# Gate and up products of 18 of 22 feature tiles made as seven block products in place of eight

## The chip, the cores and the metric

The kernel runs on one core of one Trainium2 chip. The metric is the device time of one execution in microseconds (us), the median of three runs.

## The reference

Two layers work on a state x of 512 tokens by 1024 features in float32. Each layer adds a mixer (four kinds of attention, gated and projected) and then a gated feed-forward network (FFN). The change touches the FFN alone:

```python
def rms_norm(x, g):
    y = x * lax.rsqrt(jnp.mean(x * x, axis=-1, keepdims=True) + RMS_EPS)
    return y * g

for l in range(2):
    h = rms_norm(x, g_pre_mix[l])
    x = x + rms_norm(hybrid_mixer(h, ...), g_post_mix[l])
    h = rms_norm(x, g_pre_ffn[l])
    f = (silu(h @ w_ffn_gate[l]) * (h @ w_ffn_up[l])) @ w_ffn_down[l]
    x = x + rms_norm(f, g_post_ffn[l])
```

`w_ffn_gate` and `w_ffn_up` are 1024 x 2816 and `w_ffn_down` is 2816 x 1024, so the hidden layer has 22 tiles of 128 features. `RMS_EPS` is 1e-6.

## The kernel before

State and hidden values lie feature-major: a tile is 128 features (partitions) by 512 tokens. Every float32 product is made of three products of a narrower type: an operand is split into a rounded part (hi) and the rest (lo), and `mm3` (lines 305 to 308) issues hi by hi, hi by lo and lo by hi into one PSUM bank. One feature tile of the gate or the up product (`fm`) takes 8 tiles of 128 input features, so 24 matmuls of 128 x 128 weights by 512 columns.

The weights stream in units of 128 x 1024 float32. `w_load` (line 238) issues the DMAs on SyncE (SP) into three raw buffers. `conversion` makes hi on ScalarE (line 271) and lo = raw - hi on VectorE (line 272), in two halves of 512, into two pools of four buffers; `take` hands a unit to TensorE while two more are being converted. PSUM has eight banks under two tags, `acc` and `b`, four each.

`out_block` ends with a stretch ordered by hand (`ordered(True)`), in which the first five FFN products (gate and up of tiles 0 and 1, gate of tile 2) are begun while the norm of the new state is still being formed; line 1379 makes the last of them. After it the tile scheduler sets the order, from the order of the code and the buffers.

`ffn` (lines 1385 to 1413) goes over the 22 feature tiles. The gate product in PSUM is multiplied by the norm's factors `rB` (line 1390, VectorE), goes through Silu (line 1391, ScalarE), is multiplied by `rB` again (line 1392, GpSimd: the factor of the up product), then by the up product (line 1409, VectorE), and is split into hi (line 298, ScalarE) and lo (line 299, GpSimd). The splits of all 22 tiles stay in memory until the down product: in layer 0 `down_block` goes through the 8 output tiles one after the other (`columns`, `full_column`), in layer 1 `finish` makes token-major columns of 256 with lines 792 to 794. In layer 1 `to_tokens` also transposes the state on TensorE (line 1421, copied out of PSUM by ScalarE, line 1424) in the background of the FFN.

```python
def silu(z, s, ps, rb):
    nc.vector.tensor_mul(z, ps, rb)
    nc.scalar.activation(s, z, AF.Silu)
    nc.gpsimd.tensor_mul(s, s, rb)
...
            nc.vector.tensor_mul(s, s, up)
            pr = keep(s)
            self.split_to(pr[0], pr[1], s, lo_engine=nc.gpsimd)
```

Of the kernel before, what the change touches and what calls it, by code (L numbers as in the profile page):

```python
# [17 lines left out]
S = 512  # L18
# [30 lines left out]
SQ = 3  # L49
LAST_K = ((0, 2), (2, 2), (4, 2), (6, 2), (8, 4), (12, 4), (16, 4), (20, 2))  # L50

# [6 lines left out]
def plan():  # L58
# [6 lines left out]
    for l in range(LAYERS):  # L65
# [27 lines left out]
        for m in range(FT):  # L93
            for key in ("w_ffn_gate", "w_ffn_up"):
                add(key, 8, 128, lambda a, l=l, m=m, key=key:
                    _ktiles(a[key][l], 0, 8, np.arange(m * 128, m * 128 + 128)))
        if l < LAYERS - 1:
            for d in range(8):
                for k0, nk in ((0, 8), (8, 8), (16, 6)):
                    add("down", nk, 128, lambda a, l=l, d=d, k0=k0, nk=nk:  # L100
                        _ktiles(a["w_ffn_down"][l], k0, nk, np.arange(d * 128, d * 128 + 128)))
# [92 lines left out]
class Builder:  # L194
# [28 lines left out]
    def stream_init(self):  # L223
# [5 lines left out]
        self.raw, self.whl = {}, {}  # L229

    def w_load(self, upto):
        while self.n_dma <= min(upto, len(self.plan) - 1):
            i = self.n_dma
            _, nk, nc, _ = self.plan[i]
            n = nk * nc

            t = self.a() if i < 2 else self.wraw.tile([128, 1024], F32, tag="raw", name="raw")
# [5 lines left out]
    def w_conv(self, upto):  # L243

        while self.n_conv <= min(upto, len(self.plan) - 1):
            for f in self.conversion():
                f()

    def conversion(self, lo_engine=None):
# [7 lines left out]
        if name == "held":  # L257
            tiles = [(self.ar(), self.ar()) for _ in range(2 if nk * ncol > 512 else 1)]
            if len(tiles) == 1:
                kh = nk  # L260
# [19 lines left out]
    def take(self, name, ahead=None):  # L280
# [4 lines left out]
        return self.whl.pop(i)  # L285

# [64 lines left out]
    def rms(self, ss, nt=4):  # L351

        r, steps = self.rms_steps(ss, nt)
# [4 lines left out]
    def rms_steps(self, ss, nt=4):  # L358
        v, r, t = (self.small(nt) for _ in range(3))

        def steps():
            self.nc.vector.tensor_scalar(v, ss[:, 0:nt], 1.0 / D, RMS_EPS, op0=ALU.mult, op1=ALU.add)
            yield
            yield from self.root(v, r, t)
# [482 lines left out]
    def next_factors(self, ss):  # L847
        self.rT = self.rms(ss)
# [300 lines left out]
    def columns(self, name, xs, gain, n):  # L1149

        nc = self.nc
        y, acc = [], None
        for d in range(n):
            ps = self.full_column(name, xs)
# [7 lines left out]
    def down_block(self, xs, gain, x, next_gain):  # L1162
# [29 lines left out]
        def sums(half):  # L1192
            ss[half] = self.token_sums(acc, None, 2 * half, 2)
            r[half], chain[half] = self.rms_steps(ss[half], 2)
# [190 lines left out]
    def ffn(self, l, u, ps):  # L1385
# [3 lines left out]
        def silu(z, s, ps, rb):  # L1389
            nc.vector.tensor_mul(z, ps, rb)  # L1390
            nc.scalar.activation(s, z, AF.Silu)  # L1391
            nc.gpsimd.tensor_mul(s, s, rb)  # L1392

        def keep(s):
# [203 lines left out]
```

## Time and profile before

| what | value |
|---|---|
| median of 3 runs | 1745.59 us (1744.67 to 1745.9) |
| the profiled execution, by its own clock | 1747.27 us |
| span of its profile | 1745.4 us, mean granted TensorE clock 0.994 |
| TensorE busy | 1711.2 us (98%), 9044 matmuls |
| VectorE, ScalarE, GpSimd busy | 915.2, 730.1, 468.2 us |
| moved by DMA | 179.01 MB, mean 103 GB/s |
| FFN products taken out of PSUM (lines 1390 and 1409), layer 0 / layer 1 | 529.6 to 743.9 us / 1391.9 to 1611.9 us of the span |

All durations come from the profiled execution, a single run with the profiler on, whose own time is 1.7 us above the median of the others. A matmul's row shows its start and how long it was in the array; since matmuls overlap, the distance from one start to the next (the pitch) is what one costs. "Granted clock" is the share of full speed that TensorE was given. A row of the timeline has start, duration, engine, line, operation and tiles, and in brackets how long the engine had been idle and what ended that.

### The profile page before, as it was taken

What the parts mean: (1) busy time and instruction counts of PE and PEld (TensorE: products, weight loads), DVE (VectorE), ACT (ScalarE), POOL (GpSimd) and SP (SyncE); (2) the same over time, 40 slices, a digit from 0 to 9 for tenths busy, and PEclk for the clock granted to TensorE, in tenths of its full rate; (3) what the DMA queues carried; (4) which work ended last, traced back from release to release, by engine and by line L of the source; (5) the groups of instructions that cost most, each with busy time, mean ns of one, the idle gap of its engine ahead of it and who ended that gap; (6) DMA issues with size and microseconds to landing.
All of it is one profiled execution on the core that took longest, in us unless ns stands there. A gap on an engine that the chain in (4) does not pass through costs nothing.

```text
span 1745.4 us, 24355 instructions
## 1 busy us (share of the span) xinstructions
PE 1711.2 (98%) x9044; PEld 1470.4 (84%) x9044; DVE 915.2 (52%) x1824; ACT 730.1 (42%) x1529; POOL 468.2 (27%) x420
## 2 busy tenths in 40 slices
PE   9899999999999999999998999999999999999998
PEld 7788888888898888888887888888888978888998
DVE  6767777455474333322477578665453743333223
ACT  6565653333454333323356656433234543333221
POOL 1244332211243222200233443322121432222000
PEclk9999999999999999999999999999999999999999
DMA  5544322333413333333245442223334222223321
GB/s 192 144 116 115 97 82 71 102 95 100 157 54 117 98 97 98 94 98 100 64 142 141 119 108 85 91 74 96 102 99 144 85 85 97 97 97 103 95 91 64
DMA packets 62423, 179.01 MB, mean 103 GB/s; under 512 B 8160, under 2 KB 8416, under 8 KB 62304
## 3 DMA queue, kind: packets, MB, share of 16 engines
q1 hardware_dynamic: 62304, 177.45, 33.2%
q8 instruction: 72, 1.18, 0.3%
q14 instruction: 47, 0.39, 0.1%
HBM read 156.97 MB, written 4.19 MB: 92 GB/s over the span
## 4 chain that ended last, share of the span: by engine, by line
PE 84%; DVE 6%; issue 2%; POOL 1%; ACT 1%; DMA 1%; SPq 0%; DVEq 0%; POOLq 0%; ACTq 0%
PE acc L306 21%; PE acc L308 21%; PE acc L307 21%; PE b L523 2%; PE b L443 1%; PE b L469 1%; DVE wlo L272 1%; PE b L794 1%; PE b L793 1%; PE b L792 1%; PE acc L829 1%; PE acc L831 1%; PE acc L830 1%; PE b L1480 1%; PE b L1481 1%
## 5 line engine op out<-in xcount | busy, mean ns | idle before, releaser
L306 PE MATMUL acc<-a,whi 128*128 128x512 f32 (+1 forms) x1760 | 682.4, 388 | 0.0
L308 PE MATMUL acc<-a,wlo 128*128 128x512 f32 (+1 forms) x1760 | 674.9, 384 | 0.0
L307 PE MATMUL acc<-a,whi 128*128 128x512 f32 (+1 forms) x1760 | 674.4, 383 | 0.0
L271 ACT CAST whi<-raw 128x512 fp32r<-128x512 f32 (+3 forms) x586 | 319.0, 587 | 683.1 <-issue 450.9
L272 DVE TENSOR_TENSOR wlo<-raw,whi 128x512 fp32r<-128x512 f32 (+3 forms) x582 | 399.5, 721 | 208.0 <-ACT whi L271 207.1
L308 PEld LDWEIGHTS acc<-a,wlo 128*128 128x128 f32 x1760 | 331.7, 188 | 64.6 <-issue 0.5
L307 PEld LDWEIGHTS acc<-a,whi 128*128 128x128 f32 x1760 | 332.4, 189 | 60.3 <-DVE a L302 0.6
L306 PEld LDWEIGHTS acc<-a,whi 128*128 128x128 f32 x1760 | 332.3, 189 | 59.8 <-issue 1.0
L299 POOL TENSOR_TENSOR a<-a 128x512 fp32r<-128x512 f32 (+1 forms) x80 | 114.9, 1437 | 318.9 <-ACT a L298 313.5
L1092 POOL TENSOR_TENSOR a<-a 128x512 f32<-128x512 f32 x48 | 70.5, 1470 | 247.9 <-DVE a L1091 229.2
L1073 DVE TENSOR_TENSOR a<-acc,a 128x512 f32<-128x512 f32 x64 | 44.2, 691 | 136.6 <-PE acc L308 136.5
L1392 POOL TENSOR_TENSOR a<-a 128x512 f32<-128x512 f32 x44 | 63.5, 1443 | 172.9 <-ACT a L1391 172.9
L1409 DVE TENSOR_TENSOR a<-a,acc 128x512 f32<-128x512 f32 x42 | 28.9, 687 | 139.6 <-PE acc L308 135.3
L1390 DVE TENSOR_TENSOR a<-acc,a 128x512 f32<-128x512 f32 x42 | 29.0, 691 | 134.0 <-PE acc L308 130.6
L462 POOL TENSOR_SCALAR a<-a,sm 128x128 f32<-128x128 f32 (+1 forms) x96 | 59.7, 624 | 90.8 <-DVE sm L461 66.6
L298 ACT CAST a<-a 128x512 fp32r<-128x512 f32 (+1 forms) x86 | 53.2, 618 | 66.9 <-DVE a L631 20.3
L1106 POOL TENSOR_TENSOR a<-a 128x512 f32<-128x512 f32 x26 | 35.0, 1347 | 161.8 <-ACT a L1105 161.2
L454 ACT ACTIVATE a<-a,sm 128x128 f32<-128x128 f32 (+1 forms) x96 | 53.8, 561 | 31.6 <-DVE sm L452 13.3
L480 DVE TENSOR_TENSOR ptl<-b,pth 128x128 fp32r<-128x128 f32 (+1 forms) x96 | 46.5, 486 | 31.3 <-ACT pth L479 30.9
L443 PE MATMUL b<-a 128*128 128x128 f32 (+4 forms) x224 | 51.7, 325 | 4.5 <-DVE a L742 4.4
L829 PE MATMUL acc<-whi,a 128*128 128x256 f32 x192 | 55.6, 290 | 0.0
L831 PE MATMUL acc<-whi,a 128*128 128x256 f32 x192 | 54.4, 283 | 0.0
(258 smaller groups left out, 2475.9 us busy)
## 6 DMA issues: line engine op xcount, KB each, us to landing
raw<-wts SPq DMA_DIRECT2D x242, 512.0 KB, 3.5
a<-a SPq DMA_DIRECT2D x108, 128.0 KB, 2.3
raw<-wts SPq DMA_DIRECT2D x40, 256.0 KB, 2.6
a<-xT SPq DMA_DIRECT2D x16, 256.0 KB, 5.6
raw<-wts SPq DMA_DIRECT2D x7, 452.0 KB, 3.4
a<-tab SPq DMA_DIRECT2D x12, 256.0 KB, 3.9
raw<-wts SPq DMA_DIRECT2D x8, 384.0 KB, 3.1
a<-a SPq DMA_DIRECT2D x32, 64.0 KB, 2.0
```

The source lines that it names most:

```text
L271: todo.append(lambda hi=hi, src=src, n=n: nc.scalar.copy(hi[:, :n], src))
L272: todo.append(lambda hi=hi, lo=lo, src=src, n=n: (lo_engine or nc.vector).tensor_sub(lo[:, :n], src, hi[:, :n].bitcast(F32)))
L299: (lo_engine or nc.vector).tensor_sub(lo, src, hi.bitcast(F32))
L306: mm(out, w[0], x[0], start=start, stop=False)
L307: mm(out, w[0], x[1], start=False, stop=False)
L308: mm(out, w[1], x[0], start=False, stop=stop)
L443: nc.tensor.matmul(ps[:, :L], q[:, qs], k[:, :L], start=j == 0, stop=j == len(qk[h]) - 1)
L462: nc.gpsimd.tensor_scalar(A[:, :L], A[:, :L], rr, 1.0, op0=ALU.mult, op1=ALU.mult)
L829: mm(o, x[0][:, ts], w[0][k % 4], start=k == 0, stop=False)
L831: mm(o, x[1][:, ts], w[0][k % 4], start=False, stop=k == KT - 1)
L1092: nc.gpsimd.tensor_add(merged[dd], merged[dd], t)
L1392: nc.gpsimd.tensor_mul(s, s, rb)
```

## The change

Tiles 0 to 3 stay as they were. The other 18 go in 9 groups of two tiles. In a group the gate and the up product are each seen as a 2 x 2 block product: the 1024 input features in two halves of four tiles (K blocks), the two feature tiles, and the 512 tokens in two halves of 256. Two by two blocks take eight block products; Winograd's form of Strassen's method takes seven, of sums of blocks of the weights and of sums of blocks of the activations, and adds the results up afterwards. So per group there are 7 products x 2 (gate, up) x 4 K tiles x 3 = 168 matmuls of 256 columns (`quarter_products`, new lines 465 to 467), where there were 4 x 24 = 96 of 512.

What else it does:

- **Weights.** A group's weights lie in four units, one for each block, with gate and up side by side. `units_load` brings five units for a group (new line 333, SP), and adds a second block onto two of them with an accumulating DMA issued by GpSimd (new line 335). Two further sums are made on VectorE (new line 380, 128 x 1024). Each of the seven resulting weights is converted: hi on ScalarE (new line 372), lo on VectorE (new line 373), now in one piece of 128 x 1024. Conversions run two ahead (`AHEAD`). There are 8 raw buffers instead of 3.
- **Activations.** `quarter_operands` makes the sums of the state's blocks once per layer from the state y (on VectorE 8 scalings of 128 x 512 and 16 sums of 128 x 256, then 8 splits of 128 x 512 on ScalarE and VectorE), while the last ordinary products run.
- **Results.** Some block products add on in PSUM; before the next one does, a copy is taken by ScalarE (new lines 1626 and 1633, eight of 128 x 256 in a group). VectorE adds the rest (new lines 1630 to 1655). The second multiplication by `rB` is dropped: the factor stays in the hidden layer and the norm after the FFN takes it out through a scaled epsilon (`eps`). The hidden tiles are kept whole and are split only after the FFN (`split_rest`), lo on VectorE. So GpSimd has no arithmetic left in the FFN.
- **Around it.** The state, which used to stay in SBUF, goes to DRAM and comes back (`put_away`, `bring_back`: 8 DMAs of 256 KB each way in each layer). The down product of layer 0 makes its first two output tiles side by side. The weights' order in memory follows.

The diff, cut to its core:

```diff
+CM = 4
+NR = 8
+HQ = 3
+AHEAD = 2
...
+    def units_load(self, upto):
+        nc = self.nc
+        groups = (FT - CM) // 2
+        while self.n_unit <= min(upto, 5 * groups - 1):
+            g, n = divmod(self.n_unit, 5)
+            if self.n_unit % NR < RB:
+                t = self.wraw.tile([128, 1024], F32, tag="raw", name="raw")
+            else:
+                t = self.hp.tile([128, 1024], F32, tag="fraw", name="raw")
...
+            first, more = ((a11, None), (a21, a22), (a12, None), (a11, a21), (a22, None))[n]
+            nc.sync.dma_start(t, first)
+            if more is not None:
+                nc.gpsimd.dma_start(t, more, accum_op=ALU.add)
...
+    def quarter_steps(self, u):
+        def plain(src):
+            hi = self.whi.tile([128, 1024], F32R, tag="whi", name="whi")
+            lo = self.wlo.tile([128, 1024], F32R, tag="wlo", name="wlo")
+            nc.scalar.copy(hi, src)
+            nc.vector.tensor_sub(lo, src, hi.bitcast(F32))
+            self.quarter.append((hi, lo))
+        def total(x, y, i):
+            pool, tag = ((self.wlo, "wlo"), (self.whi, "whi"))[i]
+            t = pool.tile([128, 1024], F32, tag=tag, name="sum")
+            nc.vector.tensor_add(t, x, y)
+            return t
...
+        def two():
+            p = self.unit.pop(u + 1)
+            st["q"] = total(p, self.unit.pop(u), 1)
+            plain(p)
+            self.units_load(u + 5)
+        def three():
+            st["v"] = total(st["q"], self.unit[u + 2], 0)
+            plain(st.pop("q"))
+            self.units_load(u + 6)
...
+    def quarter_operands(self, u, y, gain):
+        f = [self.a() for _ in range(KT)]
+        for k in (0, 4, 1, 5, 2, 6, 3, 7):
+            nc.vector.tensor_scalar_mul(f[k], y[k], gain(k))
...
+        for k in range(4):
+            nc.vector.tensor_sub(put(0, k), f[k][:, h0], f[k][:, h1])
+        for k in range(4):
+            stt(put(1, k), put(0, k), -1.0, f[k + 4][:, h1], op0=ALU.mult, op1=ALU.subtract)
+        split(0)
...
+        return [plain(0, h0), tiles(0), tiles(1), plain(4, h1), tiles(2), plain(4, h0), tiles(3)]
...
+    def quarter_products(self, ops, tag, done):
+        mm = self.nc.tensor.matmul
+        banks = [(self.ps(tag), self.ps(tag)) for _ in range(2)]
+        for i, x in enumerate(ops):
+            self.quarters_ahead(AHEAD)
+            hi, lo = self.quarter.popleft()
+            self.q_used += 1
+            for j in range(2):
+                chain, other = banks[j]
+                o = (chain[:, 0:256], other[:, 0:256], other[:, 256:512])[(0, 1, 0, 1, 0, 2, 0)[i]]
+                for k in range(4):
+                    c = slice(512 * j + 128 * k, 512 * j + 128 * k + 128)
+                    first = i in (0, 1, 5) and k == 0
+                    mm(o, hi[:, c], x[k][0], start=first, stop=False, skip_group_check=i in (2, 3, 4, 6))
+                    mm(o, hi[:, c], x[k][1], start=False, stop=False, skip_group_check=i in (2, 3, 4, 6))
+                    mm(o, lo[:, c], x[k][0], start=False, stop=k == 3, skip_group_check=i in (2, 3, 4, 6))
+                if i in done:
+                    done[i](j, o)
+                yield 6
...
-        for m in range(FT):
+        for m in range(CM):
             gate = ps.pop(0) if ps else (yield from self.fm("w_ffn_gate", u))
...
+            if not ps and ops is None:
+                ops = self.quarter_operands(u, y, lambda k: self.vec("pre_ffn", 8 * l + k))
+                if xt is None:
+                    self.put_away(y)
...
+            def copy(n):
+                return lambda j, o: nc.scalar.copy(e[n][:, HALF[j]], o)
+            def after_v(j, o):
+                d = (z[0], w)[j]
+                nc.vector.tensor_add(d[:, h1], o, e[2][:, HALF[j]])
+            def after_r(j, o):
+                nc.scalar.copy(e[3][:, HALF[j]], o)
+                if j == 1:
+                    nc.vector.tensor_add(e[3], e[3], e[1])
+            def after_a12(j, o):
+                d = (z[0], w)[j]
+                nc.vector.tensor_add(d[:, h0], o, e[0][:, HALF[j]])
+                if j == 0:
+                    nc.vector.tensor_mul(z[0], z[0], self.rB)
+                    nc.scalar.activation(z[0], z[0], AF.Silu)
+                    nc.vector.tensor_mul(z[1][:, h1], e[3][:, h0], self.rB[:, h1])
+                else:
+                    nc.vector.tensor_mul(z[0], z[0], w)
+                    keep(z[0])
+            def after_a22(j, o):
+                if j == 0:
+                    nc.vector.tensor_mul(z[1][:, h0], o, self.rB[:, h0])
+                    nc.scalar.activation(z[1], z[1], AF.Silu, scale=-1.0)
+                else:
+                    stt(z[1][:, h1], e[3][:, h1], -1.0, z[1][:, h1], op0=ALU.mult, op1=ALU.mult)
+                    stt(z[1][:, h0], o, -1.0, z[1][:, h0], op0=ALU.mult, op1=ALU.mult)
+                    keep(z[1])
+            yield from self.quarter_products(ops, ("acc", "b")[g % 2], {
+                0: copy(0), 1: copy(1), 2: copy(2), 3: after_v, 4: after_r, 5: after_a12, 6: after_a22})
...
+    def put_away(self, x):
+        for k in range(KT):
+            self.nc.sync.dma_start(self.away[k], x[k])
...
+    def split_rest(self, hid):
+        for m in range(FT):
+            hi = self.ar()
+            lo = self.hq.tile([128, 512], F32R, tag="h", name="h") if m >= FT - HQ else self.ar()
+            self.split_to(hi, lo, hid[m])
+            hid[m] = hi, lo
         return hid
```

The order of the instructions moves at three places. In all of them `raw` are weights as loaded, `whi` and `wlo` their hi and lo, `sum` a sum of weights made on VectorE; the numbers are the program's buffers.

The first is VectorE in the middle of the FFN of layer 0. Before, one feature tile looked like this (`a_5388` is `rB`):

```order
L1390 TENSOR_TENSOR a_6727<-acc_6702,a_5388 128x512
L272 TENSOR_TENSOR wlo_6773<-raw_6694,whi_6772 128x512 x2
L1409 TENSOR_TENSOR a_6728<-a_6728,acc_6740 128x512
L272 TENSOR_TENSOR wlo_6811<-raw_6732,whi_6810 128x512 x2
L1390 TENSOR_TENSOR a_6803<-acc_6778,a_5388 128x512
```

Now half a group of two tiles reads (`a_5394` is `rB`):

```order
L1630 TENSOR_TENSOR a_7091<-acc_7095,a_7089 128x256
L1630 TENSOR_TENSOR a_7093<-acc_7097,a_7089 128x256
L373 TENSOR_TENSOR wlo_7262<-raw_7057,whi_7261 128x1024
L380 TENSOR_TENSOR sum_7295<-raw_7104,raw_7057 128x1024
L1635 TENSOR_TENSOR a_7090<-a_7090,a_7088 128x512
L1640 TENSOR_TENSOR a_7091<-acc_7095,a_7087 128x256
L1644 TENSOR_TENSOR a_7092<-a_7090,a_5394 128x256
L1642 TENSOR_TENSOR a_7091<-a_7091,a_5394 128x512
L1640 TENSOR_TENSOR a_7093<-acc_7097,a_7087 128x256
L373 TENSOR_TENSOR wlo_7298<-raw_7104,whi_7297 128x1024
L1646 TENSOR_TENSOR a_7091<-a_7091,a_7093 128x512
L1651 TENSOR_TENSOR a_7092<-acc_7094,a_5394 128x256
```

The conversions are twice as wide and come with sums; a whole group has 9 instructions of 1024 columns, 3 of 512 and 8 of 256 on VectorE.

The second is ScalarE where the first group of layer 0 begins. Before, conversions and Silus alternated there:

```order
L271 CAST whi_5556<-raw_5478 128x512 x2
L1391 ACTIVATE a_5512<-a_5511 128x512
L271 CAST whi_5594<-raw_5516 128x512 x2
L298 CAST a_5550<-a_5512 128x512
L271 CAST whi_5632<-raw_5554 128x512 x2
```

Now (L483 splits the sums of the state, L1602 is the Silu of the last ordinary tile, and `acc_5630` and `acc_5632` are the banks of the group's first product):

```order
L372 CAST whi_5591<-raw_5515 128x1024
L483 CAST a_5487<-a_5448 128x512
L483 CAST a_5491<-a_5449 128x512
L372 CAST whi_5636<-sum_5589 128x1024
L483 CAST a_5495<-a_5450 128x512
L372 CAST whi_5669<-sum_5634 128x1024
L372 CAST whi_5699<-raw_5552 128x1024
L1602 ACTIVATE a_5586<-a_5586 128x512
L1626 COPY a_5623<-acc_5630 128x256
L1626 COPY a_5623<-acc_5632 128x256
L1626 COPY a_5624<-acc_5631 128x256
```

The copy of the first product stands behind the casts of the fourth and the fifth weight and the Silu; the third product, which adds onto the same bank, comes after it.

The third is GpSimd in the FFN of layer 0. Before, for each feature tile:

```order
L1392 TENSOR_TENSOR a_5408<-a_5408,a_5388 128x512
L299 TENSOR_TENSOR a_5414<-a_5408,a_5413 128x512
L1392 TENSOR_TENSOR a_5418<-a_5418,a_5388 128x512
L299 TENSOR_TENSOR a_5424<-a_5418,a_5423 128x512
L1392 TENSOR_TENSOR a_5428<-a_5428,a_5388 128x512
```

Now, for the whole of the FFN:

```order
L1297 TENSOR_TENSOR a_5238<-a_5238,a_5246 128x512
L335 DMA raw_5515<-wts 128x1024
L335 DMA raw_5792<-wts 128x1024
L335 DMA raw_5884<-wts 128x1024
L335 DMA raw_6036<-wts 128x1024
L335 DMA raw_6128<-wts 128x1024
```

All that is left is the accumulating DMAs, 18 in a layer; two of them (`raw_5552`, `raw_5640`) stand much earlier, among GpSimd's work for the mixer's gates, and SP issues those units' plain loads there too.

## Rows read from the trace of the kernel before

**Rows 1.** The page, part 1: busy us of each engine, share, instructions.
```profile
PE 1711.2 (98%) x9044; PEld 1470.4 (84%) x9044; DVE 915.2 (52%) x1824; ACT 730.1 (42%) x1529; POOL 468.2 (27%) x420
```

**Rows 2.** The page, part 4: the chain of work that ended last, by engine.
```profile
PE 84%; DVE 6%; issue 2%; POOL 1%; ACT 1%; DMA 1%; SPq 0%; DVEq 0%; POOLq 0%; ACTq 0%
```

**Rows 3.** Windows: two FFN stretches of 512 columns, one of 256, one with heavy loading.
```profile
core 0: us, PE busy (x) PEld busy (x) DVE busy (x) ACT busy (x) POOL busy (x), PEclk, DMA share, GB/s
560.00:600.00 40.00, 40.00 (x179) 33.11 (x178) 14.11 (x23) 12.07 (x22) 12.08 (x8) 1.00 0.31 93
1560.00:1600.00 40.00, 40.00 (x178) 33.14 (x177) 13.24 (x21) 11.69 (x21) 11.05 (x8) 1.00 0.32 105
1640.00:1680.00 40.00, 40.00 (x336) 40.00 (x335) 12.85 (x24) 11.93 (x32) 0.00 (x0) 1.00 0.28 86
910.00:920.00 10.00, 7.82 (x40) 6.48 (x40) 6.54 (x15) 5.07 (x10) 0.34 (x1) 1.00 0.78 259
```

**Rows 4.** Timeline of PE, layer 0 FFN: 24 matmuls of 512 columns apart.
```profile
600.18 0.39 PE L306 MATMUL acc<-a,whi 128*128 128x512 f32 x1
...
605.62 0.39 PE L306 MATMUL acc<-a,whi 128*128 128x512 f32 x1
```

**Rows 5.** Timeline of PE, layer 1 down product: 35 matmuls of 256 columns apart.
```profile
1639.78 0.28 PE L793 MATMUL b<-wlo,h 128*128 128x256 f32 x1
...
1643.98 0.28 PE L792 MATMUL acc<-whi,a 128*128 128x256 f32 x1
```

**Rows 6.** Groups by line and shape, 560 to 800 us: busy us, mean ns.
```profile
L272 DVE TENSOR_TENSOR wlo<-raw,whi 128x512 fp32r<-128x512 f32 x82 | 53.3, 689 | 25.3 <-ACT whi L271 25.3
...
L271 ACT CAST whi<-raw 128x512 fp32r<-128x512 f32 x80 | 46.0, 619 | 147.2 <-issue 123.9 <-PE acc L307 23.4
...
L1391 ACT ACTIVATE a<-a 128x512 f32<-128x512 f32 x17 | 10.7, 629 | 0.1
```

**Rows 7.** Groups by line and shape, the whole run.
```profile
L272 DVE TENSOR_TENSOR wlo<-raw,whi 128x512 fp32r<-128x512 f32 x484 | 357.4, 773 | 165.0 <-ACT whi L271 164.3
...
L271 ACT CAST whi<-raw 128x256 fp32r<-128x256 f32 x72 | 25.7, 405 | 102.6 <-issue 79.9 <-PE acc L307 15.9 <-PE b L794 6.5
...
L1115 DVE TENSOR_TENSOR a<-a,b 128x256 f32<-128x256 f32 x48 | 19.0, 410 | 2.6 <-PE b L371 2.6
```

**Rows 8.** Timeline of DVE at the beginning of the layer 0 FFN.
```profile
533.93 0.68 DVE L272 TENSOR_TENSOR wlo<-raw,whi 128x512 fp32r<-128x512 f32 x1
534.53 0.68 DVE L1390 TENSOR_TENSOR a<-acc,a 128x512 f32<-128x512 f32 x1
...
543.77 3.07 DVE L272 TENSOR_TENSOR wlo<-raw,whi 128x512 fp32r<-128x512 f32 x2 [0.49 <-ACT whi L271]
```

**Rows 9.** The page, part 6: DMA issues, KB each, median us to landing.
```profile
raw<-wts SPq DMA_DIRECT2D x242, 512.0 KB, 3.5
...
a<-xT SPq DMA_DIRECT2D x16, 256.0 KB, 5.6
```

**Rows 10.** Timeline, all engines, where the layer 0 FFN begins.
```profile
520.49 1.02 PE L347 MATMUL b<-ct,a 128*128 128x1 f32 x8 [0.88 <-DVE a L844]
...
521.58 0.41 PE L1248 MATMUL acc<-a,wlo 128*128 128x256 f32 x1
...
521.79 0.41 PE L1247 MATMUL acc<-a,whi 128*128 128x256 f32 x1
...
525.11 0.40 PE L306 MATMUL b<-a,whi 128*128 128x512 f32 x1
```

**Rows 11.** Windows: the granted clock (third from the end) over 520 to 530 us.
```profile
520.00:530.00 10.00, 9.51 (x52) 8.83 (x53) 6.69 (x16) 4.45 (x9) 0.00 (x0) 0.83 0.51 154
```

**Rows 12.** Timeline of PE, layer 1: two waits at the transposes of the state.
```profile
1403.05 1.15 PE L1421 MATMUL b<-ct,a 128*128 128x128 f32 x8 [0.41 <-ACT a L1424]
1405.21 0.66 PE L1421 MATMUL b<-ct,a 128*128 128x128 f32 x4 [1.02 <-DVE a L1409]
```

More of the change, by code (lines that the diff above doesn't have):

```diff
@@ L257, in conversion @@
         if name == "held":
-            tiles = [(self.ar(), self.ar()) for _ in range(2 if nk * ncol > 512 else 1)]
-            if len(tiles) == 1:
-                kh = nk
+            kh = nk
+            if self.n_held < 2:
+                t2 = self.hp.tile([128, 1024], F32R, tag="fraw", name="held")
+                tiles = [(t2[:, 0:512], t2[:, 512:1024])]
+            else:
+                tiles = [(self.ar(), self.ar())]
+            self.n_held += 1
         else:
@@ new lines, in quarters_ahead, with quarters_init @@
+    def quarters_ahead(self, n):
+        while self.q_todo and self.q_done <= n + self.q_used:
+            self.q_todo.popleft()()
+            self.q_done += 1
+        if not self.q_todo:
+            self.n_conv = max(self.n_conv, self.q_end)
+            self.w_conv(self.q_end + n + self.q_used - self.q_done)
+    def quarters_init(self):
+        groups = (FT - CM) // 2
+        self.q_todo, self.q_done, self.q_used = deque(), 0, 0
+        self.quarter = deque()
+        self.unit, self.n_unit = {}, 0
+        self.q_end = self.wi + 4 * groups
+        while self.plan[self.q_end - 4 * groups][0] != "quarter":
+            self.q_end += 1
+        for g in range(groups):
+            self.q_todo.extend(self.quarter_steps(5 * g))
@@ new lines, in quarter_steps, with one, four, five @@
+    def quarter_steps(self, u):
+        nc = self.nc
+        st = {}
+        def plain(src):
[9 more added lines that the diff above has]
+            return t
+        def one():
+            self.units_load(u + 4)
+            plain(self.unit[u])
+        def two():
[7 more added lines that the diff above has]
+            self.units_load(u + 6)
+        def four():
+            plain(st.pop("v"))
+        def five():
+            plain(self.unit.pop(u + 3))
+            self.units_load(u + 7)
+        def six():
+            plain(self.unit.pop(u + 2))
+        def seven():
+            plain(self.unit.pop(u + 4))
+        return [one, two, three, four, five, six, seven]
@@ L1152, in columns @@
         y, acc = [], None
+        ready = []
+        if name == "down":
+            ready = [self.ps("acc"), self.ps("acc")]
+            k0 = 0
+            while k0 < len(xs):
+                w = [self.take(name, CL - i) for i in range(2)]
+                nk = len(w[0][0])
+                for k in range(k0, k0 + nk):
+                    for i in range(2):
+                        self.mm3(ready[i], (w[i][0][k - k0], w[i][1][k - k0]), xs[k], k == 0, k == len(xs) - 1)
+                k0 += nk
         for d in range(n):
-            ps = self.full_column(name, xs)
+            ps = ready.pop(0) if ready else self.full_column(name, xs)
             acc = self.add_square(acc, ps, nc.gpsimd)
@@ L1408, in ffn @@
             up = ps.pop(0) if ps else (yield from self.fm("w_ffn_up", u, "b" if m == 2 else "acc"))
[L1409 to L1411 removed]
+            nc.vector.tensor_mul(z, z, up)
+            keep(z)
             yield 3
+        if xt is not None:
+            self.drain("xt")
+            self.put_away([xt[t, h] for t in range(4) for h in range(2)])
+            xt.clear()
+        del y
+        h0, h1 = HALF
```

133 lines of the change are left out of this document (96 added, 37 removed).

## The prediction

> **What bounds the kernel now.** I read the page first, then the windows of the FFN, then the timeline of single engines. TensorE is busy for 98% of the span [rows 1] and carries 84% of the chain that ended last [rows 2]. The windows say the same of the stage that is changed: in 40 us of either layer's FFN TensorE is busy for 40.00 at a granted clock of 1.00, while VectorE works 14, ScalarE 12 and GpSimd 12 us [rows 3]. So in the FFN the time is the number of matmuls times their pitch, and a change pays there by what it takes off that product, less any wait that it puts in.
>
> The pitch comes from the timeline. From 600.18 to 605.62 us there are 24 matmuls of 512 columns: 5.44 / 24 = 0.2267 us [rows 4]. From 1639.78 to 1643.98 us there are 35 of 256 columns: 4.20 / 35 = 0.1200 us [rows 5]; the window around it has 336 in 40 us, which is the same [rows 3]. Two matmuls of 256 columns thus cost 0.240 us where one of 512 costs 0.2267: narrow matmuls give back 5.9% of what fewer of them save.
>
> **The sum, TensorE.** A group of two feature tiles had 96 matmuls of 512 columns: 96 x 0.2267 = 21.76 us. It has 168 of 256 now: 168 x 0.1200 = 20.16 us. That is 1.60 us a group; 9 groups in each of 2 layers make 28.8 us. The saving is 7%, not the eighth that seven products for eight suggest.
>
> Here a rule can be weighed against the two pitches [rows 4, 5]. The Trainium skill, "TensorE: Matmul & The Clock Gate", section Back-to-back issue gap, gives an isolated gap of N / 2.4 + 2.5 ns, which would be 215.8 and 109.2 ns, and a saving of 18 x (20.72 - 18.35) = 43 us. The trace disagrees: both pitches are about 11 ns longer here, and that counts more on the narrow one. The rows decide.
>
> **What the other engines must do in a group's 20.16 us.** No operation of 1024 columns is in the trace, so I extend those for 512 and 256 [rows 6, 7]. On VectorE 512 columns take 689 ns and 256 take 410, so 1024 take about 689 + 2 x 279 = 1247 ns; instructions in a row overlap by 0.08 us (0.68 long, 0.60 apart [rows 8]), so 1.17 us each. Nine of 1024, three of 512 (0.60) and eight of 256 (0.33) make 10.5 + 1.8 + 2.6 = 14.9 us, 74% of the group. As upper bound I take the whole run's mean of 773 ns for 512, which has GpSimd working beside it in other stages: 9 x 1.55 + 3 x 0.69 + 8 x 0.41 = 19.3 us, 96%. I take 14.9: the 773 is made by stretches such as 543.77 us, where a pair of 512 beside GpSimd took 3.07 us [rows 8], and the change leaves GpSimd no arithmetic in the FFN.
>
> On ScalarE 512 columns take 619 ns and 256 take 405, so 1024 about 1047. Seven of these, eight copies of 256 and two Silus of 629 ns make 7.3 + 3.2 + 1.3 = 11.8 us, 59%. Both fit. Seven transfers of 512 KB a group are 3.67 MB in 20.16 us, 182 GB/s; the window at 910 us moved 259 at a DMA share of 0.78 [rows 3], so bytes alone are no bound. The 16 extra transfers of the state in each layer are off every path: each 256 KB took up to 5.6 us [rows 9], and what comes back is wanted only at the end of the down product.
>
> **The accumulating DMA.** Nothing in the trace before shows one. A plain transfer of 512 KB lands in 3.5 us, and 256 KB of the first ones, when the queue was crowded, in 5.6 [rows 9]. Below: 3.5 us. Above: twice the slow one for twice the bytes, 11.2 us. In the steady order a group's plain load is issued about one group ahead, so some 20 us are there for plain load (3.5) and addition; I take a value well under 16 us, which costs nothing. The two that GpSimd issues early, among the mixer's gates, make GpSimd wait for a plain load; that stage's work behind it is not waited for by TensorE in a way I can price, and I put 0 on it, with 1 us above.
>
> **Where the start of the groups waits.** The gate of tile 2 begins at 525.11 us [rows 10] and ends near 531.5; three ordinary products of 5.44 follow, so the first block product P0 of layer 0 can begin at about 547.8 and end 24 x 0.12 = 2.9 us later, at 550.7. On ScalarE the cast of the fourth weight must wait for a buffer that P0 reads until then; the order shows it, the next cast and a Silu ahead of the copy of P0's result. They end at 550.7 + 1.05 + 1.05 + 0.63 = 553.4, the copy at 553.8, while the third product, which adds onto P0's bank, is due after 12 matmuls of the second, at 552.1. So TensorE waits about 1.8 us once. A wait of that sort has a price behind it: before, after 0.88 us of waiting at 520.49, 256-column matmuls came 0.21 us apart instead of 0.12 [rows 10], half clock (1.2 GHz in place of 2.4), until shortly before 525.11, and the granted clock of that window is 0.83 [rows 11], 1.7 us lost in 10. I put 1.5 us for it here. In steady state the copies have 2.9 us from the end of a product to the next use, and ScalarE is 59% busy, so nothing waits.
>
> In layer 1 the state's transposes stand at that place. They already wait 0.41 and 1.02 us for ScalarE and VectorE [rows 12], and the copies now compete with more casts: plus 1.0 us. At the end of the FFN the last group's hidden tiles are split after their Silu, where before one tile's split was left: 0.5 us a layer, 1.0 in all; the other tiles' splits (at most 1.0 us each on ScalarE and VectorE, with the conversion of their weights) fit beside the 6 x 0.2267 = 1.36 us of products for each.
>
> Sum: -28.8 + 1.8 + 1.5 + 1.0 + 1.0 = -23.5 us. The profiled execution took 1747.27 us, 1.7 above the median of the runs; against it the changed kernel takes 1723.8, and against the median of 1745.6, about **1722 us**.
>
> **The rivals.** A measurement of this kernel tells about 0.2% from no change, so 3.5 us: faster is under 1742.1, slower over 1749.1.
>
> 1. *The forecast*, TensorE stays the bound of the groups: 1722, from 1715 (no start-up waits at all, and the 1.4 us of idle before the transposes gone [rows 12]) to 1729 (each of them twice as large). TensorE's 40.00 of 40 us in the FFN [rows 3] and the 74% speak for it. Chance 0.66.
> 2. *VectorE becomes the bound.* The group's 14.9 us become more than 20.16 once a 1024-column instruction costs (20.16 - 5.0) / 9 = 1.68 us. For it: the whole run's mean gives 1.55, near to that, and VectorE works in order, so that a sum that waits for an accumulating DMA holds up the results of the group. Against it: the 689 of the FFN. At 1.75 us a group takes 20.75, 0.6 longer; 18 of these are 11 us and the time 1733. Chance 0.16.
> 3. *The accumulating DMA becomes the bound, and the kernel is slower.* GpSimd issues two in a group, and if the second starts only when the first has landed, a group takes the larger of 20.16 us and 2d. From d = 10.1 us it costs, and from 2d = 21.5 (the old 21.76 less start-up costs of 5.3 / 18 = 0.3), d = 10.7, the kernel is slower than before. At the upper bound of 11.2 us a group takes 22.4, which is 0.64 over the old one: 18 x 0.64 + 5.3 = 17 and 1762 us. For it: a read and a write of the buffer for each byte, and no row that shows the operation. Against it: the 3.5 us of a plain one. Chance 0.10. The Trainium skill, "DMA: Bandwidth & Descriptors", section SWDGE vs HWDGE vs iDMA, speaks against the change in this place: only GpSimd can issue such a transfer, by writing its descriptors into memory that VectorE can lock it out of. Section Anatomy of one DMA of the same page fits 2.0 us plus bytes at 436 GB/s, which would be 3.2 us, an estimate from that page and for a plain transfer. No run here shows either yet.
> 4. *The change does not do what it says*: the blocks' matmuls run slower than the 256-column ones of before [rows 5], because chain and second bank alternate and each product changes its weights and its operand. From 21.76 / 168 = 0.1295 us the products gain nothing; with the start-up costs the time is 1746 to 1751. Against it: those rows too take a new weight and another operand from one matmul to the next. Chance 0.05.
>
> 0.03 is left for what I do not see.
>
> **How the numbers follow.** The predicted time is that of the first case. The range reaches from 1714 to the end of the second case and a little over it, 1741: that is about 0.82. The two cases are faster; a tenth of the second lies over 1742.1. Faster 0.82, within 0.2% 0.06 (the fourth and the edge of the second), slower 0.12 (the third, part of the fourth, and what I do not see).
>
> **What would show it.** In the profile after, TensorE has 9044 + 2 x 9 x 72 = 10,340 matmuls. In the middle of the FFN the matmuls of lines 465 to 467 should start 0.120 us apart without gaps, and windows of 20 us should show PE at 20.00, VectorE near 15 and ScalarE near 12. The accumulating DMAs should land in under 16 us, with two in each 20.16 us. At the first group of layer 0 there should be a wait of TensorE for the copies of line 1626, of about 2 us, with a stretch of half clock behind it. I am wrong if a 1024-column VectorE instruction takes over 1.68 us, if sums (line 380) wait for DMA, if the pitch is over 0.125, or if the wait at the start of a group comes back in every group.

## The result, and the profile after

The changed kernel takes 1714.16 us (median of 4 runs, 1712.14 to 1716.85) where the kernel before takes 1745.13 (1743.64 to 1745.9): a ratio of 0.9825, 95% interval 0.9806 to 0.9843, which is 27 to 34 us less. The prediction was 1722 us, in a range of 1714 to 1741: the sign and what bounds the kernel were right, the gain was put at 23.5 us and is about 31, and the median lies only 0.2 us inside the range. The profiled execution took 1716.04 us with a span of 1714.3, so 31.1 us less span than before, at the same mean granted clock of 0.994.

The page, part 1, of the changed kernel, to be held against [rows 1]:

```profile
PE 1680.4 (98%) x10340; PEld 1507.9 (88%) x10340; DVE 1104.0 (64%) x2080; ACT 832.3 (49%) x1671; POOL 368.6 (21%) x368
```

There are the 10,340 matmuls that were forecast; 1296 more take 30.8 us less of TensorE. VectorE has 189 us more work, ScalarE 102 more, GpSimd 100 less. Two windows in the FFN, one in each layer, with the columns of [rows 3]:

```profile
600.00:680.00 80.00, 80.00 (x669) 80.00 (x668) 61.50 (x80) 42.69 (x68) 6.92 (x8) 1.00 0.72 184
1440.00:1520.00 80.00, 80.00 (x669) 80.00 (x669) 61.04 (x79) 42.72 (x68) 6.92 (x8) 1.00 0.75 184
```

TensorE is busy for 80.00 of 80 us; VectorE for 77% of it and ScalarE for 53%. The DMA share more than doubled, from 0.31 and 0.32 to 0.72 and 0.75, while the GB/s went from 93 and 105 to 184. The groups by line and shape show what the new instructions take, over the whole run:

```profile
L373 DVE TENSOR_TENSOR wlo<-raw,whi 128x1024 fp32r<-128x1024 f32 x90 | 110.3, 1225 | 57.1 <-ACT whi L372 53.8 <-PE acc L467 1.8
...
L372 ACT CAST whi<-raw 128x1024 fp32r<-128x1024 f32 x90 | 94.5, 1050 | 95.2 <-PE acc L466 47.0
...
L335 POOL DMA_DIRECT2D raw<-wts x36 | 31.3, 870 | 344.5 <-DMA raw<-wts 180.1 <-ACT whi L372 25.0 <-DVE a L1630 20.9
...
L380 DVE TENSOR_TENSOR sum<-raw 128x1024 f32<-128x1024 f32 x18 | 22.0, 1225 | 9.1 <-PE acc L466 4.6 <-PE b L466 4.6
```

The 1024-column instructions take 1225 ns on VectorE and 1050 on ScalarE, where the prediction had extended 1247 and 1047 from 512 and 256 columns. Issuing an accumulating DMA takes GpSimd 0.87 us, which the prediction had left out; GpSimd has the time. The page, parts 3 and 6, for the DMAs:

```profile
q1 hardware_dynamic: 69504, 195.28, 36.6%
q0 software_dynamic: 5184, 18.88, 6.7%
...
raw<-wts SPq DMA_DIRECT2D x260, 512.0 KB, 3.6
raw<-wts POOLq DMA_DIRECT2D x36, 512.0 KB, 6.1
```

An accumulating DMA (on q0, issued by GpSimd) lands in 6.1 us, between the bounds of 3.5 and 11.2 us. Where the time went is read from the timeline of TensorE. Its rows here are the first block product of layer 0, the first matmul after the last block product, the gate of tile 2 in layer 1 and the end of that FFN:

```profile
545.23 0.28 PE L465 MATMUL acc<-a,whi 128*128 128x256 f32 x1
...
728.40 0.40 PE L491 MATMUL acc<-a,whi 128*128 128x512 f32 x1
...
1372.04 0.40 PE L491 MATMUL b<-a,whi 128*128 128x512 f32 x1
...
1580.46 0.28 PE L983 MATMUL b<-whi,a 128*128 128x256 f32 x1
```

Before, layer 1 went from 1386.42 to 1611.58 us:

```profile
1386.42 0.63 PE L306 MATMUL b<-a,whi 128*128 128x512 f32 x1
...
1611.58 0.28 PE L792 MATMUL b<-whi,a 128*128 128x256 f32 x1
```

| stretch | before | after | difference |
|---|---|---|---|
| layer 0, 18 tiles (1512 matmuls now, 864 x 0.2267 before) | 195.9 | 183.2 | -12.7 |
| layer 1, gate of tile 2 to the end of the FFN | 225.2 | 208.4 | -16.7 |
| end of that FFN to the end of the span | 133.8 | 133.8 | 0.0 |
| everything else | 1190.5 | 1188.9 | -1.6 |

### The profile page after: what moved, and what is told of

Read it like the earlier page. It is cut to its first block, busy times and chain, and to the rows that moved or that the text cites. A ratio compares the mean times of both kernels' runs of the same rounds, so it can differ in the third digit from the quotient of the medians.

```text
span 1714.3 us, 27427 instructions
## 1 busy us (share of the span) xinstructions
PE 1680.4 (98%) x10340; PEld 1507.9 (88%) x10340; DVE 1104.0 (64%) x2080; ACT 832.3 (49%) x1671; POOL 368.6 (21%) x368
## 3 DMA queue, kind: packets, MB, share of 16 engines
q1 hardware_dynamic: 69504, 195.28, 36.6%
q0 software_dynamic: 5184, 18.88, 6.7%
## 4 chain that ended last, share of the span: by engine, by line
PE 60%; DVE 5%; ACT 1%; issue 1%; POOL 1%; DMA 0%; DVEq 0%; SPq 0%; ACTq 0%; POOLq 0%
PE acc L491 8%; PE acc L492 8%; PE acc L493 8%; PE acc L465 4%; PE acc L467 4%; PE acc L466 4%; PE b L467 3%; PE b L466 3%; PE b L465 3%; PE b L983 1%; PE b L985 1%; PE b L984 1%; PE b L714 1%; DVE wlo L298 1%; PE b L634 1%
## 5 line engine op out<-in xcount | busy, mean ns | idle before, releaser
L491 PE MATMUL acc<-a,whi 128*128 128x512 f32 (+1 forms) x1238 | 478.3, 387 | 0.0
L493 PE MATMUL acc<-a,wlo 128*128 128x512 f32 (+1 forms) x1238 | 470.5, 380 | 0.0
L492 PE MATMUL acc<-a,whi 128*128 128x512 f32 (+1 forms) x1211 | 460.1, 380 | 0.0
L298 DVE TENSOR_TENSOR wlo<-raw,whi 128x512 fp32r<-128x512 f32 (+3 forms) x438 | 302.3, 721 | 179.1 <-ACT whi L297 177.7
L465 PE MATMUL acc<-a,whi 128*128 128x256 f32 x560 | 158.6, 283 | 1.9 <-DVE a L1601 1.5
L466 PE MATMUL acc<-a,whi 128*128 128x256 f32 x560 | 158.4, 283 | 0.0
L467 PE MATMUL acc<-a,wlo 128*128 128x256 f32 x560 | 158.3, 283 | 0.0
L373 DVE TENSOR_TENSOR wlo<-raw,whi 128x1024 fp32r<-128x1024 f32 x90 | 110.3, 1225 | 57.1 <-ACT whi L372 53.8
L372 ACT CAST whi<-raw 128x1024 fp32r<-128x1024 f32 x90 | 94.5, 1050 | 95.2 <-PE acc L466 47.0
L465 PE MATMUL b<-a,whi 128*128 128x256 f32 x448 | 126.8, 283 | 0.0
L466 PE MATMUL b<-a,whi 128*128 128x256 f32 x448 | 126.8, 283 | 0.0
L467 PE MATMUL b<-a,wlo 128*128 128x256 f32 x448 | 126.8, 283 | 0.0
L1283 POOL TENSOR_TENSOR a<-a 128x512 f32<-128x512 f32 x48 | 70.5, 1469 | 237.8 <-DVE a L1282 229.1
```

Source lines behind the costliest of these rows:

```text
L298: todo.append(lambda hi=hi, lo=lo, src=src, n=n: (lo_engine or nc.vector).tensor_sub(lo[:, :n], src, hi[:, :n].bitcast(F32)))
L372: nc.scalar.copy(hi, src)
L373: nc.vector.tensor_sub(lo, src, hi.bitcast(F32))
L465: mm(o, hi[:, c], x[k][0], start=first, stop=False, skip_group_check=i in (2, 3, 4, 6))
L466: mm(o, hi[:, c], x[k][1], start=False, stop=False, skip_group_check=i in (2, 3, 4, 6))
L467: mm(o, lo[:, c], x[k][0], start=False, stop=k == 3, skip_group_check=i in (2, 3, 4, 6))
```

## The experiments

**Both kernels once more, for the clock.** No edit. The question was whether the stretches of half clock belong to places of the program.

> The kernel before, once more, for a second profile. Theory (the stretches of half clock fall by chance): the 18 matmuls between the norm's sum and the gate of tile 2, which took 3.73 us in layer 0 and 2.79 in layer 1, take 2.24 us (full clock) in at least one of the two layers, and the profile's other stretches of half clock lie elsewhere than at 55, 85, 520, 875, 955 and 1385 us. Rival (they belong to the place): the same stretches at the same places. Time 1743 to 1747 us either way.

> The changed kernel, once more. Median 1712 to 1717 us, ratio to before 0.981 to 0.984. Theory (half clock by chance): its stretches of half clock move to other places, and the 18 matmuls before the gate of tile 2 may be slow in one layer. Rival (the change keeps the clock up there): those 18 take 2.24 us in both layers again. In both, the second product of the first group of layer 0 waits about 1.7 us for VectorE's line 1601.

The changed kernel: 1714.88 us, ratio 0.9829 (0.9815 to 0.9844). The kernel before: 1747.48 us in its one run. Timeline of TensorE of the repeated kernel before, the 18 matmuls before the gate of tile 2, and the window around them:

```profile
522.67 0.36 PE L1247 MATMUL acc<-a,whi 128*128 128x256 f32 x1
...
524.90 0.40 PE L306 MATMUL b<-a,whi 128*128 128x512 f32 x1
```

```profile
520.00:530.00 10.00, 9.12 (x61) 8.19 (x60) 8.07 (x18) 4.77 (x9) 0.00 (x0) 1.00 0.47 135
...
920.00:925.00 5.00, 5.00 (x26) 4.82 (x27) 3.67 (x5) 4.64 (x9) 1.28 (x1) 0.66 0.57 157
```

They take 2.23 us at a granted clock of 1.00, where the first profile had 3.73 us and 0.83 [rows 10, 11], though the same wait of 0.88 us stands ahead of them. In exchange a stretch at 920 us is at 0.66, where the first profile showed none. So a wait may be followed by half clock (1.2 GHz) or not, in the same program. The first profile of before was longer by 1.5 us at this place in layer 0 and by as much in layer 1 (0.55 in those 18 matmuls, 1.0 in the gate of tile 2 behind them); this is no gain of the change.

In the repeated changed kernel the 18 matmuls take 2.23 and 2.24 us in the two layers, as the rival (the change keeps the clock up there) would have it. But two runs below, which are the changed kernel with one edit, are slow there: 3.73 us in layer 1 of the run without accumulating DMA, 3.43 us in layer 0 of the run with seven lo parts made twice. So the change does not by itself keep the clock up. Other stretches (near 85 us in both kernels, near 860, 905 and 942 us in the changed one) come back at their places, so the theory of chance holds for the two places that the account needs, and not for all. The wait of 1.7 us at the first group of layer 0 comes back as expected.

**One and five groups in place of nine.**

```diff
-CM = 4
+CM = 20
```

> One group of block products in each layer in place of nine; everything else of the change stays. Theory (each group saves 1.60 us, the rest of the change saves 2 to 3 us or nothing): 2 x 1.60 = 3.2 us from the products, so 1739 to 1742 us. Rival (the fixed costs are the 5.3 us of the prediction and the profiled run was lucky): 1744 to 1748 us. Second rival (the gain comes from the relief of GpSimd and the new banks, not from fewer columns): under 1735 us.

```diff
-CM = 4
+CM = 12
```

> Five groups of block products in each layer in place of nine. Theory (the gain is linear in the groups, 1.60 us each): 8 x 1.60 = 12.8 us above the changed kernel, 1725 to 1730 us. Rival (the weights' loads and conversions of a long row of groups fall behind, so that the later groups cost more than the first): less than 10 us above it.

One group: 1739.66 us, ratio 0.9969 (0.9958 to 0.9981). Five groups: 1725.67 us, ratio 0.9885 (0.9868 to 0.9901). Between one group and nine a layer lie 16 groups: 1739.66 - 1714.5 = 25.2 us, 1.57 a group (1714.5 lies between the two medians of the changed kernel, 1714.16 and 1714.88). The first eight of them bring 14.0 us and the other eight 11.2. Timeline of TensorE in the kernel with one group, where that group begins and ends in layer 0:

```profile
720.66 0.28 PE L465 MATMUL acc<-a,whi 128*128 128x256 f32 x1
...
740.81 0.40 PE L491 MATMUL acc<-a,whi 128*128 128x512 f32 x1
```

20.15 us for 168 matmuls, without a wait; the five groups take 100.8 us for 840 in each layer. The forecast of 20.16 holds for every group, and the gain is linear in the groups as far as the medians tell. The kernel with one group is 3 to 7 us faster than before where its products save 3.2: in its layer 1 the transposes wait no longer, which is 1.8 us (below).

**Matmuls of 256 columns alone.** The kernel before, with the 18 tiles in two halves of tokens:

```diff
...
+        if narrow:
+            for hs in HALF:
+                for k in range(nk):
+                    self.mm3(ps[:, hs], (w[0][k], w[1][k]), [p[:, hs] for p in x[k]], k == 0, k == nk - 1)
...
```

> The kernel before, with the gate and up products of tiles 4 to 21 made in two halves of 256 tokens: 1728 matmuls of 256 columns a layer in place of 864 of 512, still eight block products. Theory (the pitch of 0.1200 us is what counts): 2 x (207.4 - 195.9) = 23.0 us more than before, 1766 to 1770, so that seven for eight is worth 51.8 us and the narrow matmuls take 23.0 of it back. Rival (two matmuls of 256 cost no more than one of 512 in this loop, and the changed kernel saves for another reason): 1743 to 1749.

1765.4 us, ratio 1.012 (1.0103 to 1.0136): 18 to 24 us slower, where the pitch says 23.0; the median is just under the expected 1766. In layer 0 its 1728 narrow matmuls take 207.4 us, as forecast. Window of this run:

```profile
600.00:680.00 80.00, 80.00 (x669) 80.00 (x669) 26.48 (x42) 23.47 (x42) 19.66 (x14) 1.00 0.27 91
```

669 matmuls in 80 us, just as in the changed kernel's windows. So seven products in place of eight of the same width are worth about 51 us (1765.4 - 1714.5), and the narrower matmuls take some 21 of them back.

**No accumulating DMA.** VectorE makes the two sums, from four loads a group:

```diff
-            first, more = ((a11, None), (a21, a22), (a12, None), (a11, a21), (a22, None))[n]
-            nc.sync.dma_start(t, first)
-            if more is not None:
-                nc.gpsimd.dma_start(t, more, accum_op=ALU.add)
+            first = (a11, a21, a12, None, a22)[n]
+            if first is not None:
+                nc.sync.dma_start(t, first)
...
+            nc.vector.tensor_add(self.unit[u + 3], self.unit[u], self.unit[u + 1])
...
+            nc.vector.tensor_add(p, p, self.unit[u + 4])
...
```

> No accumulating DMA: VectorE makes the two sums as well, from four loads in place of seven transfers a group. Theory (TensorE bounds the group, VectorE has room): VectorE 17.2 us of 20.16 in a group, time within 3 us of the changed kernel, 1711 to 1718. Rival (VectorE, working in order, is at its limit and the DMA sums are what keeps it off the path): TensorE waits in each group, 5 to 20 us more, 1720 to 1735.

1716.25 us, ratio 0.9837 (0.9822 to 0.9852), which can't be told from the changed kernel's. Its window:

```profile
600.00:680.00 80.00, 80.00 (x669) 80.00 (x668) 69.19 (x88) 43.05 (x68) 0.00 (x0) 1.00 0.32 104
```

VectorE is busy for 86% and still off the path; the DMA share falls back from 0.72 to 0.32. The gain needs no accumulating DMA.

**VectorE loaded further.** The lo part of four weights of a group, or of all seven, is made twice:

```diff
-            nc.vector.tensor_sub(lo, src, hi.bitcast(F32))
+            for _ in range(2 if len(st.setdefault("lo", [])) < 4 else 1):
+                nc.vector.tensor_sub(lo, src, hi.bitcast(F32))
+            st["lo"].append(0)
```

> The lo part of four of a group's seven weights is made twice by VectorE (the second time into the same tile): 4 x 1.16 us more, 19.6 us of 20.16 in a group. Theory (VectorE's room is 20.16 less 14.9 us and waits of single instructions are absorbed): no change beyond 3 us, 1711 to 1719. Rival (it works in order and cannot use the last quarter): TensorE waits 1 us or more in each of 18 groups, 1730 or above.

> The lo part of all seven weights of a group is made twice: 7 x 1.16 us more, 23.0 us of work for VectorE in a group. Theory: the group takes VectorE's 23.0 us in place of TensorE's 20.16, 18 x 2.8 = 51 us more, 1760 to 1770. Rival (the groups were already held by VectorE in part): 18 x 8.1 = 146 us more, 1850 or above.

Four: 1724.84 us, ratio 0.9885 (0.9868 to 0.9902), 10 us above the changed kernel, between the two expectations. Seven: 1783.85 us, ratio 1.0234 (1.0215 to 1.0254), 69 us above it, between the two as well. The edit moves the lines of the conversion and of the matmuls by one and two. TensorE's timeline with four, and with seven:

```profile
615.00 0.28 PE L468 MATMUL b<-a,whi 128*128 128x256 f32 x1
615.51 0.39 PE L469 MATMUL b<-a,wlo 128*128 128x256 f32 x1 [0.22 <-DVE wlo L374]
```

```profile
651.27 0.58 PE L469 MATMUL acc<-a,wlo 128*128 128x256 f32 x1 [1.62 <-DVE wlo L374]
651.65 0.42 PE L467 MATMUL acc<-a,whi 128*128 128x256 f32 x1
651.87 0.42 PE L468 MATMUL acc<-a,whi 128*128 128x256 f32 x1
```

and their windows of 600 to 680 us:

```profile
600.00:680.00 80.00, 79.08 (x653) 78.27 (x652) 76.13 (x95) 42.73 (x66) 6.91 (x8) 1.00 0.68 178
```

```profile
600.00:680.00 80.00, 70.84 (x551) 69.14 (x550) 76.78 (x90) 38.14 (x58) 5.19 (x6) 0.96 0.57 146
```

With 19.6 us of work TensorE loses 0.4 us in every group but the first of a layer, at one lo that VectorE has not finished (16 x 0.4 = 6 us), and more at the start; at 95% VectorE is already on the path. With seven it is the bound: 3.85 us more a group, 24.0 us, of which 23.0 are its work. The forecast had left out the rest: VectorE's own waits, and matmuls 0.22 us apart (half clock) after the long waits, as from 651.65 to 651.87 us. So the second rival begins to show with 4 more instructions of 1024 columns a group.

**The accumulating DMA twice.**

```diff
-                nc.gpsimd.dma_start(t, more, accum_op=ALU.add)
+                for _ in range(2):
+                    nc.gpsimd.dma_start(t, more, accum_op=ALU.add)
```

> Each accumulating DMA is issued twice, four in a group, the second after the first has landed (the added block is then in the sum twice, so another product is computed). Theory (6.1 us each, and GpSimd waits for two of the four): about 14 us of the group's 20.16, no change beyond 3 us, 1711 to 1718. Rival (the transfers are near their limit, or slow the plain loads beside them): TensorE waits for sums in each group, 4 x 6.1 = 24.4 us a group, 1780 to 1795.

1722.16 us, ratio 0.9868 (0.9843 to 0.9892): 7 to 8 us more than the changed kernel, so neither expectation. Windows of both layers, and ScalarE's timeline at the longest of the waits:

```profile
600.00:680.00 80.00, 76.83 (x641) 76.62 (x639) 57.15 (x76) 39.19 (x63) 11.36 (x13) 1.00 0.86 211
1440.00:1520.00 80.00, 80.00 (x669) 80.00 (x668) 59.09 (x77) 43.28 (x68) 12.19 (x14) 1.00 0.91 223
```

```profile
678.92 1.04 ACT L373 CAST whi<-raw 128x1024 fp32r<-128x1024 f32 x1 [5.23 <-DMA raw<-wts]
```

In most groups TensorE waits for nothing, but at a DMA share of 0.86 to 0.91 single units of weights land late: here ScalarE waits 5.23 us for one, a copy behind that cast is late, and TensorE loses 3.6 us; a second place of 2.8 us lies in layer 1. GpSimd's timeline ahead of that place, and the landings of its DMAs from 640 to 682 us:

```profile
655.96 1.75 POOL L336 DMA_DIRECT2D raw<-wts  x2 [10.03 <-DMA raw<-wts]
668.07 1.75 POOL L336 DMA_DIRECT2D raw<-wts  x2 [10.35 <-DMA raw<-wts]
681.03 1.75 POOL L336 DMA_DIRECT2D raw<-wts  x2 [11.21 <-DMA raw<-wts]
...
raw<-wts POOLq DMA_DIRECT2D x8, 512.0 KB, 10.6
```

A row is two issues: the second addition to one unit and the first to the next. Ahead of each, GpSimd waits 10 to 11 us for its own last addition to land; over the whole run it does so 31 times, 250 us in all, and never in the changed kernel. So the third rival's mechanism is seen here as the prediction had it, GpSimd issuing one after the other: 10.6 us is over its limit of 10.1, and 2 x 10.6 is over the 20.16 of a group, so that the units fall behind until ScalarE waits. That the additions take 10.6 us, where the changed kernel's between 600 and 680 us take 6.5, goes with the DMA share; no run separates its cause.

**The wait at the first group.** First in both layers, then in layer 0 alone, the gate and up products of tile 3 go to the other four banks. The edit for layer 0 alone:

```diff
-            gate = ps.pop(0) if ps else (yield from self.fm("w_ffn_gate", u))
+            gate = ps.pop(0) if ps else (yield from self.fm("w_ffn_gate", u, "b" if xt is None else "acc"))
...
-            up = ps.pop(0) if ps else (yield from self.fm("w_ffn_up", u, "b" if m == 2 else "acc"))
+            up = ps.pop(0) if ps else (yield from self.fm("w_ffn_up", u, "b" if m == 2 or xt is None else "acc"))
```

> The gate and up products of tile 3 go to the other four PSUM banks, so that no bank of the first group waits for VectorE to empty it. Theory (two waits lie one behind the other): the 1.7 us at the second product vanish, and the third product waits 1.3 to 1.6 us for ScalarE's copy of the first (line 1626) instead, as the prediction had it; time unchanged within 1 us in the stage. Rival (the copy is in time): the stage is 1.7 us shorter and no wait of TensorE over 0.3 us is left in it.

> As the run with the other banks, but in layer 0 only, where no transposes use them. Theory (a first group that need not wait for VectorE to empty a bank finds ScalarE's copy in time): the 1512 matmuls of layer 0 take 181.6 us in place of 183.2, layer 1 is as in the changed kernel, and the time is 1.6 us under it, 1711 to 1715 by median. Rival (the wait turns up at another place of the stage): 183 us and no gain.

In both layers: 1720.77 us in one run. The wait in layer 0 is gone, and none follows, so the rival was right there: 1512 matmuls in 181.6 us. But in layer 1, where the transposes use the same four banks, the order changed and TensorE waits 4.4 us:

```profile
1389.27 0.58 PE L467 MATMUL acc<-a,wlo 128*128 128x256 f32 x1 [4.37 <-DVE wlo L373]
```

In layer 0 alone: 1712.66 us, ratio 0.9813 (0.9798 to 0.9828). Its first group starts and its last one ends at

```profile
542.86 0.28 PE L465 MATMUL acc<-a,whi 128*128 128x256 f32 x1
...
724.47 0.40 PE L491 MATMUL acc<-a,whi 128*128 128x512 f32 x1
```

181.6 us, as expected, and layer 1 is as in the changed kernel. It is the fastest version by median; the 1.6 us are shown by the trace of the stage, while the medians' intervals overlap.

## Why the prediction was right, and where it was off

**The products: right to the digit.** 0.1200 us for a matmul of 256 columns, 20.16 us for a group, 28.8 us in all; one group, five and nine agree with it, and so does the run with narrow matmuls. By the Trainium skill's isolated gap ("TensorE: Matmul & The Clock Gate", Back-to-back issue gap) the estimate would have been 0.109 us and 43 us; the runs decide for the rows.

**VectorE and ScalarE: right.** 15.5 us and 10.8 us a group by the windows (61.50 and 42.69 of 80), against 14.9 and 11.8. The second rival fell, and the loaded runs show how much room there was: at 86% of VectorE TensorE still works 80.00 of 80 us, at 95% it loses 0.4 us in nearly every group. The rival's threshold is loose: its 5.0 us for the other instructions is 4.4 in the prediction's own sum, which makes the threshold 1.75 us and not 1.68; nothing hangs on it at a measured 1.225.

**The accumulating DMA: right that it costs nothing here.** 6.1 us was inside the bounds and under the 10.1 from which the third rival had it cost; with four additions a group the 10.6 us are over it, and cost follows. The estimate for a plain transfer from the Trainium skill's fit ("DMA: Bandwidth & Descriptors", Anatomy of one DMA), 3.2 us, is half of the 6.1. Of VectorE locking GpSimd out in its 2-port mode (the Trainium skill, same page, section SWDGE vs HWDGE vs iDMA) the trace shows nothing: the 36 issues take 856 to 1023 ns each, beside a VectorE busy for 77%; whether any of VectorE's instructions ran in that mode, the trace does not tell.

**The wait at the first group of layer 0: the size right, the cause wrong.** The prediction had ScalarE's copy late by 1.8 us. TensorE waited 1.68, but at the second product, for a bank that VectorE had still to empty. Timeline of TensorE, of VectorE and of ScalarE there:

```profile
547.98 0.28 PE L467 MATMUL acc<-a,wlo 128*128 128x256 f32 x1
549.78 0.35 PE L465 MATMUL acc<-a,whi 128*128 128x256 f32 x1 [1.52 <-DVE a L1601]
549.98 0.28 PE L466 MATMUL acc<-a,whi 128*128 128x256 f32 x1
```

```profile
547.21 1.22 DVE L373 TENSOR_TENSOR wlo<-sum,whi 128x1024 fp32r<-128x1024 f32 x1
548.35 0.68 DVE L484 TENSOR_TENSOR a<-a 128x512 fp32r<-128x512 f32 x1
548.95 0.68 DVE L1601 TENSOR_TENSOR a<-acc,a 128x512 f32<-128x512 f32 x1
```

```profile
550.66 0.62 ACT L1626 COPY a<-acc 128x256 f32<-128x256 f32 x2
```

Line 1601 multiplies the gate of tile 3, whose bank the second product takes. VectorE, without a pause since it began the sums of the state, comes to it 9 us after the gate product was done. The prediction had followed ScalarE's queue only. That queue it had right: the copy of the first product starts at 550.66 us, 2.7 us after that product's last matmul, but the wait for the bank covers it. In this order, with the third product due 1.44 us after the first, the copy would have held TensorE about 1.5 us by itself, an estimate from these rows. With the bank free (the runs with the other banks) the copy is just in time, because the third product then comes behind both halves of the second.

**The half clock behind it: wrong.** Put at 1.5 us; from 549.98 us on the matmuls are 0.12 us apart again.

**Layer 1: wrong in sign.** Put at 1.0 us more. The first group waits 0.5 us there, but the two waits of [rows 12], 1.8 us with what they cost around them, are gone, in the changed kernel and with one group a layer. In the kernel before, VectorE's line 1409, for which the transposes waited, stood behind a pair of conversions that took 3.05 us beside GpSimd's multiplication. Timelines of VectorE and GpSimd of the kernel before:

```profile
1401.51 3.05 DVE L272 TENSOR_TENSOR wlo<-raw,whi 128x512 fp32r<-128x512 f32 x2 [0.61 <-ACT whi L271]
1404.48 0.68 DVE L1409 TENSOR_TENSOR a<-a,b 128x512 f32<-128x512 f32 x1
```

```profile
1402.61 1.40 POOL L1392 TENSOR_TENSOR a<-a 128x512 f32<-128x512 f32 x1 [0.28 <-ACT a L1391]
```

The change takes GpSimd's arithmetic out of the FFN, and with it, as I read these rows, what held VectorE there. That this alone removed the waits was not tried by itself.

**The end of the FFN: wrong.** Put at 1.0 us; in layer 0 TensorE goes on without a wait, and behind layer 1's FFN the stretch is 133.8 us in both.

So the step that failed is the sum of start-up costs: 5.3 us in the prediction, and 1.7 + 0.5 - 1.8 = 0.4 measured. -28.8 + 0.4 = -28.4 us, inside the interval of -27 to -34. It fits the table: layer 0 is -14.4 + 1.7 = -12.7, layer 1 is -14.4 + 0.5 - 1.8 - 1.0 = -16.7, of which the 1.0 is half clock. The profiled pair shows 31.1; about 3 us of that are the two stretches of half clock which only the first profile of before has at these places. But the second profile of before, with its half clock elsewhere, is as long (1745.7 us). So the rest of the medians' 31 us, 2.6, is not explained by these two places; it is within the interval and stays open.

That the time fell inside the range owes something to luck. Its lower end of 1714 lies 1 us under the case of no start-up waits and no idle before the transposes (1715); the median is 1714.16, and two of the four runs, 1712.14 and 1712.29, lie below. The term that carries the forecast, -28.8 us, is no luck. Two readings of the prediction are loose besides, and the forecast rests on neither: 1729, the upper end of the first case, counts from the profiled 1747.27 us and would be 1727 from the median, and the 5.6 us of [rows 9] are a median and not the longest transfer.

## What to carry to other kernels

A matmul's pitch at both widths, read from one's own trace, priced the products of this change to the digit: by the runs, seven products for eight saved some 51 us and half the width took 21 back. For the start of such a stage follow every engine's queue to the operations that free a bank, not only those that feed the products. When one engine issues DMAs that must land one after the other, hold the time to landing, under the load of that stage, against the time between them. And a stretch of half clock that two runs of the same kernel do not share belongs in no account of a change.

## What had not been expected of the hardware

- **Accumulating costs the DMA engines twice a plain transfer.** In the changed kernel 18.88 MB took 6.7% of 16 engines' span and 195.28 MB took 36.6%: 0.067 x 1714.3 / 18.88 = 6.1 us a MB against 3.2. Hence the share of 0.72 at only 184 GB/s, and 0.91 at 223 with two more a group, where plain loads had 0.78 at 259 [rows 3].
- **Half clock moves.** With the same wait of 0.88 us ahead, the same 18 matmuls ran at 0.83 in the window once and at 1.00 another time; two of the changed kernel's four runs had a mean granted clock of 0.998 and took 1712.14 and 1712.29 us, the other two had 0.994 and 0.995 and took 1716.04 and 1716.85.
